# A router's chain rebuilt: logits by token, slots from a triangular matrix, a shorter first gather

## The chip, the cores and the metric

The kernel runs on one core of a Trainium2 chip. The metric is the device time of one execution in microseconds. The engines are TensorE (PE, with PEld for its weight loads), VectorE (DVE), ScalarE (ACT), GpSimd (POOL) and SyncE (SP), which issues the loads of the weights.

## The reference

Two transformer-like blocks run one after the other on 256 tokens of width 1024. The change lies in the first block, between its mixer and its experts:

```python
x = x + merged @ w_o[l]
h = rmsnorm(x, g_ffn[l])
aff = jax.nn.softmax((h @ w_router[l]).astype(f32), axis=-1)     # 256 tokens x 16 experts
vals, idx = lax.top_k(jnp.swapaxes(aff, 1, 2), cap)              # cap = 32 tokens for each expert
xe = h[bidx, idx]
gt = jnp.einsum('becd,edf->becf', xe, w_gate[l])
up = jnp.einsum('becd,edf->becf', xe, w_up[l])
ye = jnp.einsum('becf,efd->becd', jax.nn.silu(gt) * up, w_down[l])
ye = ye * vals[..., None].astype(ye.dtype)
x = x + jnp.zeros_like(x).at[bidx, idx].add(ye.astype(dt))
```

Each of the 16 experts picks its 32 tokens of highest affinity, and three f32 matrices of 1024x2048 (8 MB each) are applied to them. Every weight is read once.

## The kernel before

Tokens lie on partitions, in two tiles of 128; `s.x` holds x as 128 x 2 x 1024. A scheduler places the instructions of each engine in an order of its own; within one engine they then run strictly in that order.

**The end of the mixer.** `w_o(b)` multiplies with one half of w_o's columns, in four pieces, through `lin_A_steps`. Each piece makes 12 matmuls, and the last adds the result to `s.x` (L863). Three pieces into `w_o(1)`, `router_start` and `router_half(0)` come in between: the transposes of x (L896), their copies to `xT` by ScalarE (L897) and VectorE (L898), and the logits (L900). `router_half(1)` does the same for the other four channel tiles once `w_o(1)` is added.

**The router, in `moe`.** The sum of squares and its power -0.5 (`rs`, on POOL, L359) run beside the logits. The logits, 16 x 256 with experts on partitions, are copied (L926) and transposed (L931); softmax (L933 to L942) has tokens on partitions; the affinities are transposed back (L947) and copied (L949). Four rounds of MAX, which finds eight at a time, and three replacements between them (L953, L955) give each expert's 32nd value, the threshold. A token above it gets a slot: two running sums along the tokens (L965), for those above and for those equal to the threshold, are masked and added (L966, L967) and transposed (L970), and `pos` (L972) holds the slot of each token with each expert. `onehot` (L979) compares `pos` with `iota` and makes for each expert two matrices of 128 x 32, for two token tiles: `oh` with rs in it gathers, `wt` with the affinity scatters.

**Gather and experts.** `gather(g, ks, lo, hi)` multiplies the channel tiles `ks` of x with `oh` (L997) and VectorE writes the product times g_ffn to `xe` (L1000). For expert 0 it is called for tiles (0, 1) and (2, 3) first, then the one-hots of all the other experts are written, then the experts run. Expert e takes for each of eight channel tiles k one chunk of w_gate and one of w_up (L1017), then eight chunks of w_down (L1041). In expert 0, `gather` is called for tiles (4, 5) after k=1 and for (6, 7) after k=3, and after w_down for all the other experts.

**The loads.** `wload` (L915, and L919 in two halves) issues on SyncE's queue one DMA for each chunk of 128 x 2048 f32, 1 MB. Its buffers stand in the list `RING2`, 18 of them, with two more (`SPARE`) once. A chunk's load waits until its buffer's last reader is done. The first 20 buffers come free as the mixer ends; load 21 is the first that reuses a buffer of the experts themselves, that of expert 0's w_gate, k=0, and so on in turn: loads 21 to 24 reuse the chunks of k=0 and k=1, load 25 that of w_gate, k=2. Load 43 reuses the buffer of load 25, which is expert 1's w_gate, k=0.

Of the kernel before, what the change touches and what calls it, by code (L numbers as in the profile page):

```python
# [242 lines left out]
class Net:  # L243
# [201 lines left out]
            if next(e[3], StopIteration) is StopIteration:  # L445
                live.remove(e)

    def lin_A_steps(s, aps, xT, kts, evac, cols=512):

        pss = [s.bank([P, cols], name=f"lA{t}") for t in range(2)]  # L450
        n = 0

        def halves():
            for ap in aps or []:
                w = s.wload2(ap, ap.shape[1])
                for a in range(0, ap.shape[1], 2 * cols):
                    yield s.wsplit(w[:, a:a + 2 * cols])
            while aps is None and n < kts:
                yield s.piece()
        for p in halves():  # L460
            h, l = [v.rearrange("p (k c) -> p k c", c=cols) for v in p]
            for i, (w, x) in enumerate(((h, xT[0]), (h, xT[1]), (l, xT[0]))):
                for kk in range(2):
                    for t in range(2):
                        s.nc.tensor.matmul(pss[t], x[:, n + kk, t * P:t * P + P], w[:, kk, :],  # L465
                                           start=n + kk + i == 0, stop=i == 2 and n + kk == kts - 1)
            n += 2
            if n == kts:
                for t in range(2):
                    evac(t, pss[t])  # L470
            yield
# [11 lines left out]
    def mixer(s):  # L483
        nc, A, vec = s.nc, s.A, s.nc.vector
# [38 lines left out]
        r = s.rstd_halves(s.x)  # L523
# [4 lines left out]
        for b in range(2):  # L528
            cs = slice(512 * b, 512 * b + 512)
# [329 lines left out]

        def w_o(b):  # L860
            def evac(t, ps):
                xv = s.x[:, t, 512 * b:512 * b + 512]
                vec.tensor_tensor(xv, xv, ps, op=OP.add)  # L863
            return s.lin_A_steps(None, mm, 8, evac)
        run(w_o(0))
        last = w_o(1)
        for _ in range(3):
# [20 lines left out]
    def router_half(s, b):  # L888

        nc = s.nc  # L890
        for kp in (2 * b, 2 * b + 1):
            ps = s.trb([P, 2, T])
            for j in range(2):
                k = 2 * kp + j
                for t in range(2):
                    nc.tensor.transpose(ps[:, j, t * P:(t + 1) * P], s.x[:, t, k * P:(k + 1) * P], s.ident)  # L896
            nc.scalar.copy(s.xT[:, 2 * kp, :], ps[:, 0, :])  # L897
            nc.vector.tensor_copy(s.xT[:, 2 * kp + 1, :], ps[:, 1, :])  # L898
        for k in range(4 * b, 4 * b + 4):
            nc.tensor.matmul(s.logits, s.gw[:, k, :], s.xT[:, k, :], start=k == 0, stop=k == KT - 1)  # L900

    def moe(s):
        nc, A = s.nc, s.A
# [4 lines left out]
        def wload(ap):  # L908
# [13 lines left out]
        nc.gpsimd.iota(iota, pattern=[[1, C]], base=1, channel_multiplier=0,  # L922
                       allow_small_or_imprecise_dtypes=True)
        r = s.rstd_halves(s.x)
        lg = s.tmp([E, T])
        nc.scalar.copy(lg, s.logits)  # L926


        pl = s.trb([P, 2, E])
        for t in range(2):  # L930
            nc.tensor.transpose(pl[:, t, :], lg[:, t * P:(t + 1) * P], s.ident[:E, :E])  # L931
        mx = s.sm.tile([P, 2], F32, name="mx", bufs=1)
        nc.vector.tensor_reduce(mx, pl, axis=AX, op=OP.max, negate=True)  # L933
        nc.vector.tensor_tensor(mx, mx, r, op=OP.mult)
        aff = s.slot("hsd01", "aff", [P, 2, E], tag="hsd01")
        sm = s.sm.tile([P, 2], F32, name="smx", bufs=1)
        for t in range(2):
            nc.scalar.activation(aff[:, t, :], pl[:, t, :], AF.Exp, scale=r[:, t:t + 1], bias=mx[:, t:t + 1],
                                 accum_out=sm[:, t:t + 1])
        nc.vector.reciprocal(sm, sm)  # L940
        for t in range(2):
            nc.vector.tensor_scalar(aff[:, t, :], aff[:, t, :], sm[:, t:t + 1], None, op0=OP.mult)  # L942
# [13 lines left out]
        thr = m8[:, 7:8]  # L956
        above, equal = [s.tmp([E, 2, T]) for _ in range(2)]
        cnt = s.sm.tile([E, 1], F32, name="cnt", bufs=1)
        ones = s.slot("hsd11", "ones16", [E, T], tag="hsd11")
        nc.gpsimd.memset(ones, 1.0)  # L960
        nc.vector.tensor_scalar(above[:, 0], at, thr, 0.0, op0=OP.is_gt, op1=OP.add, accum_out=cnt)
        nc.vector.tensor_scalar(equal[:, 0], at, thr, None, op0=OP.is_equal)
# [5 lines left out]
        pslot = s.trb([P, 2, E])  # L968
# [3 lines left out]
        nc.vector.tensor_copy(pos, pslot)  # L972

        ohwt = s.slot("K0", "ohwt", [P, 2, 2, E, C])
        oh, wt = ohwt[:, 0], ohwt[:, 1]
# [8 lines left out]
        def gather(g, ks, lo, hi):  # L984

            kk = ks[0] // 4
            if (g, kk) not in xe:
                if g == 0:
                    xe[g, kk] = s.slot("", "xe", [P, 4, 4 * C], tag=("dft", "dft0")[kk])
                else:  # L990
                    both = s.slot(("K1", "X")[g // 3], "xe", [P, 2, 2, 4, 4 * C])
                    xe.update({(i, j): both[:, i - g, j] for i in (g, g + 1) for j in range(2)})
            n = hi - lo
            ps = s.bank([P, len(ks), n * C])
            for i, k in enumerate(ks):
# [14 lines left out]
        for e in range(E):  # L1010
            es = slice(e % 4 * C, (e % 4 + 1) * C)
            pg, pu = s.bank([P, 512]), s.bank([P, 512])
            for k in range(KT):
                for w, ps in (("w_gate", pg), ("w_up", pu)):
                    c = wload(A[w][e, k])
                    for j in range(4):
                        nc.tensor.matmul(ps[32 * j:32 * j + 32, :], xe[e // 4, k // 4][:, k % 4, es],  # L1017
                                         c(j), start=k == 0, stop=k == KT - 1)
                if e == 0 and k in (1, 3):
                    gather(0, (k + 3, k + 4), 0, 1)  # L1020
            pp = s.trb([P, T])
            for t in range(2):
                rep = s.tmp([P, 4, C])
# [838 lines left out]
```

## Time and profile before

| | |
|---|---|
| time, median of 3 runs | 2606.54 us (2606.51 to 2606.96) |
| time of the profiled execution | 2609.32 us |
| its span | 2607.3 us |
| TensorE busy | 2261.8 us, 87% |
| VectorE busy | 1160.5 us, 45% |
| ScalarE busy | 843.2 us, 32% |
| POOL busy | 226.1 us, 9% |
| moved from HBM | 661.92 MB, 254 GB/s over the span |

The profile is that of one execution. Its times count from the start of the span. Busy shares are means over stages of quite different kinds: the mixer ends at about 360 us, the router lies between 360 and 379, the experts follow to about 1290, and the second block takes the rest. TensorE's clock has two levels, and the profile gives the granted share: 1.00 is 2.4 GHz, 0.50 is 1.2 GHz.

### The profile page before, as it was taken

How to read it: one execution, taken by the hardware profiler on the slowest of the kernel's cores; microseconds unless marked ns; L12 is line 12 of the kernel's file. 1: busy time of each engine (PE TensorE's matmuls, PEld its weight loads, DVE VectorE, ACT ScalarE, POOL GpSimd, SP SyncE). 2: the span in 40 equal slices, each digit the busy share in tenths (PEclk: the TensorE clock that was granted, in tenths of full speed). 3: DMA queues.
4: the chain of work that ended last, by engine and by line, in shares of the span. 5: the costliest groups of instructions: out<-in, count | busy, mean ns of one | idle time of the engine just before them, and what ended most of it. 6: DMA issues, size and time to landing. Idle time of an engine off the chain costs nothing.

```text
span 2607.3 us, 33443 instructions
## 1 busy us (share of the span) xinstructions
PE 2261.8 (87%) x13686; PEld 1506.8 (58%) x13686; DVE 1160.5 (45%) x1700; ACT 843.2 (32%) x1299; POOL 226.1 (9%) x250
## 2 busy tenths in 40 slices
PE   7999889767676677677799999999999999989999
PEld 6988854111111111111288887788888888768887
DVE  6886861000000000000265587555555557765554
ACT  4653320000000000000244455355444445545543
POOL 3321300000000000000000041100000005110000
PEclk9999989877778878787799999999999999999999
DMA  5343679999999999999955524245555553424553
GB/s 199 130 146 139 234 281 423 425 426 425 426 425 427 425 426 425 426 425 426 390 195 184 181 96 159 82 162 179 192 179 192 172 175 121 146 80 168 186 180 127
DMA packets 104633, 665.14 MB, mean 255 GB/s; under 512 B 11808, under 2 KB 12192, under 8 KB 34848
## 3 DMA queue, kind: packets, MB, share of 16 engines
q1 hardware_dynamic: 103328, 660.12, 65.4%
q8 instruction: 107, 1.75, 0.3%
q10 hardware_dynamic: 1008, 1.84, 0.2%
q0 software_dynamic: 144, 1.05, 0.1%
q14 instruction: 46, 0.38, 0.0%
HBM read 661.92 MB, written 1.05 MB: 254 GB/s over the span
## 4 chain that ended last, share of the span: by engine, by line
PE 54%; DMA 33%; DVE 8%; ACT 2%; issue 2%; POOL 1%; SPq 0%; DVEq 0%; ACTq 0%; POOLq 0%
PE lA L465 32%; DMA wc<-in_w_down_dram 13%; DMA wc<-in_w_up_dram 13%; PE acc L430 8%; DMA wc<-in_w_gate_dram 5%; PE lA L1670 2%; DVE wl L308 2%; DMA wc<-in_x_wkv_dram 1%; PE trb L1070 1%; ACT wh L307 1%; PE acc L1017 1%; PE acc L313 1%; PE acc L997 1%; PE acc L315 1%; PE acc L314 1%
## 5 line engine op out<-in xcount | busy, mean ns | idle before, releaser
L308 DVE TENSOR_TENSOR wl<-wc,wh 128x1024 fp32r<-128x1024 f32 (+1 forms) x447 | 550.2, 1234 | 376.9 <-ACT wh L307 365.9
L307 ACT CAST wh<-wc 128x1024 fp32r<-128x1024 f32 (+1 forms) x454 | 471.9, 1041 | 553.5 <-PE lA L465 405.2
L1017 PE MATMUL acc<-wc,xe 128*32 128x512 f32 x2048 | 371.1, 769 | 177.1 <-DMA wc<-in_w_up_dram 92.6
L1017 PEld LDWEIGHTS acc<-wc,xe 128*32 128x32 f32 x2048 | 52.5, 120 | 482.4 <-DMA wc<-in_w_up_dram 220.7
L1030 DVE TENSOR_TENSOR tmp<-tmp,acc 128x512 f32<-128x512 f32 x16 | 11.0, 687 | 530.0 <-PE acc L1017 521.8
L465 PE MATMUL lA<-wh,hTl 128*128 128x512 f32 (+1 forms) x864 | 236.4, 390 | 0.0
L465 PE MATMUL lA<-wh,hTh 128*128 128x512 f32 (+1 forms) x864 | 231.3, 388 | 3.4 <-ACT hTh L373 3.4
L465 PE MATMUL lA<-wl,hTh 128*128 128x512 f32 (+1 forms) x864 | 227.8, 385 | 2.6 <-DVE wl L308 2.6
L1041 PE MATMUL acc<-wc,tmp 128*32 128x512 f32 x1024 | 170.0, 745 | 64.4 <-DMA wc<-in_w_down_dram 50.6
L465 PEld LDWEIGHTS lA<-wh,hTh 128*128 128x128 f32 x864 | 161.9, 189 | 35.8 <-ACT hTh L373 5.2
L465 PEld LDWEIGHTS lA<-wl,hTh 128*128 128x128 f32 x864 | 161.9, 189 | 34.0 <-DVE wl L308 3.7
L1029 ACT ACTIVATE tmp<-acc 128x512 f32<-128x512 f32 x16 | 9.6, 597 | 512.6 <-PE acc L1017 512.6
L465 PEld LDWEIGHTS lA<-wh,hTl 128*128 128x128 f32 x864 | 159.0, 189 | 26.5
L1054 DVE TENSOR_TENSOR x<-x,acc 128x512 f32<-128x512 f32 x64 | 44.0, 688 | 263.3 <-PE acc L1053 263.3
L1041 PEld LDWEIGHTS acc<-wc,tmp 128*32 128x32 f32 x1024 | 30.5, 125 | 187.2 <-DMA wc<-in_w_down_dram 100.1
L1050 ACT COPY tmp<-acc 128x512 f32<-128x512 f32 x32 | 18.8, 586 | 313.8 <-PE acc L1041 313.8
L465 PE MATMUL lA<-wl,hidh 128*128 128x512 f32 x352 | 96.1, 391 | 0.0
L465 PE MATMUL lA<-wh,hidh 128*128 128x512 f32 x352 | 94.4, 390 | 0.0
L465 PE MATMUL lA<-wh,hidl 128*128 128x512 f32 x352 | 94.1, 389 | 0.0
L430 PE MATMUL acc<-hTh,wl 128*128 128x256 f32 x544 | 81.1, 290 | 10.4 <-DVE wl L308 10.2
L430 PE MATMUL acc<-hTh,wh 128*128 128x256 f32 x544 | 86.5, 299 | 1.5 <-ACT wh L307 1.0
L1024 POOL COPY tmp<-ohwt 128x128 f32<-128x128 f32 x32 | 9.4, 296 | 847.2 <-PE trb L1033 668.5
(448 smaller groups left out, 3073.1 us busy)
## 6 DMA issues: line engine op xcount, KB each, us to landing
wc<-in_w_up_dram SPq DMA_DIRECT2D x117, 1024.0 KB, 18.4
wc<-in_w_gate_dram SPq DMA_DIRECT2D x102, 1024.0 KB, 19.4
wc<-in_w_down_dram SPq DMA_DIRECT2D x102, 1024.0 KB, 18.3
wc<-in_ffn_wi_dram SPq DMA_DIRECT2D x88, 1024.0 KB, 4.8
wc<-in_ffn_wo_dram SPq DMA_DIRECT2D x40, 1024.0 KB, 4.8
wc<-in_w_in_dram SPq DMA_DIRECT2D x39, 1024.0 KB, 4.8
wc<-in_w_gate_dram SPq DMA_DIRECT2D x52, 512.0 KB, 13.5
wc<-in_w_down_dram SPq DMA_DIRECT2D x52, 512.0 KB, 15.9
```

The source lines that it names most:

```text
L307: s.nc.scalar.copy(h[:, :n], w)
L308: (eng or s.nc.vector).tensor_tensor(l[:, :n], w, h[:, :n].bitcast(F32), op=OP.subtract)
L313: mm(out, a[0], b[0], start=start, stop=False)
L314: mm(out, a[0], b[1], start=False, stop=False)
L315: mm(out, a[1], b[0], start=False, stop=stop)
L430: s.nc.tensor.matmul(ps[:, c, :], w[:, k, :], x[:, k, :], start=i + k == 0, stop=i == len(terms) - 1 and k == KT - 1)
L465: s.nc.tensor.matmul(pss[t], x[:, n + kk, t * P:t * P + P], w[:, kk, :], start=n + kk + i == 0, stop=i == 2 and n + kk == kts - 1)
L997: nc.tensor.matmul(ps[:, i, :], s.x[:, t, k * P:(k + 1) * P], oh[:, t, 4 * g + lo:4 * g + hi].rearrange("p e c -> p (e c)"), start=t == 0, ...
L1017: nc.tensor.matmul(ps[32 * j:32 * j + 32, :], xe[e // 4, k // 4][:, k % 4, es], c(j), start=k == 0, stop=k == KT - 1)
L1041: nc.tensor.matmul(py[b][32 * j:32 * j + 32, :], ht[:, t, 32 * j:32 * j + 32], c(j), start=t == 0, stop=t == 3)
L1054: nc.vector.tensor_tensor(s.x[:, t, cs], s.x[:, t, cs], ps, op=OP.add)
L1670: s.nc.tensor.matmul(pss[t], x[:, n + kk, t * P:t * P + P], w_[:, kk, :], start=n + kk + i == 0, stop=i == 2 and n + kk == KT - 1)
```

## The change

Five things change, all between the mixer's last matmuls and expert 0.

- In the last piece of `w_o(1)` the six matmuls of token tile 0 come first and are added, then those of tile 1, which is added in two halves of 256 columns.
- The logits are computed with tokens on partitions: xT is the stationary operand, the 16 columns of gw the moving one. The copy, the first pair of transposes and the copy of the transposed affinities go away. Softmax runs for one token tile after the other.
- The threshold is transposed and spread over all partitions, and two comparisons write `sel` (above, equal) as bf16 with tokens on partitions. The slots come from products of `sel` with a triangular matrix of ones (`upto`) and a full one, in place of the running sums.
- `iota` moves behind the router's chain, into the buffer of `gw`; its old place is taken by the making of `upto`.
- Before expert 0 only the channel tiles (0, 1) are gathered; (2, 3), (4, 5) and (6, 7) are called after k=0, k=2 and k=4.

```diff
@@ lin_A_steps
+            terms = [(w, x, i, kk) for i, (w, x) in enumerate(((h, xT[0]), (h, xT[1]), (l, xT[0]))) for kk in range(2)]
+            last = in_turn and n + 2 == kts
+            for ts, part in ([((t,), terms) for t in range(2)] if last else [((0, 1), [u]) for u in terms]):
+                for w, x, i, kk in part:
+                    for t in ts:
                         s.nc.tensor.matmul(pss[t], x[:, n + kk, t * P:t * P + P], w[:, kk, :],
                                            start=n + kk + i == 0, stop=i == 2 and n + kk == kts - 1)
+                if last:
+                    evac(ts[0], pss[ts[0]])
@@ router_start
-        s.logits = s.bank([16, T])
+        s.logits = [s.bank([P, 16], name=f"lg{t}") for t in range(2)]
+        s.upto = s.slot("hsd00", "upto", [P, 2, P], BF16, tag="hsd00")
+        nc.gpsimd.memset(s.upto[:, 1], 1.0)
+        ramp = s.slot("hsd01", "ramp", [P, P], tag="hsd01")
+        nc.gpsimd.iota(ramp, pattern=[[1, P]], base=0, channel_multiplier=-1, allow_small_or_imprecise_dtypes=True)
+        nc.gpsimd.tensor_scalar(s.upto[:, 0], ramp, 0.0, None, op0=OP.is_ge)
@@ router_half
-        for k in range(4 * b, 4 * b + 4):
-            nc.tensor.matmul(s.logits, s.gw[:, k, :], s.xT[:, k, :], start=k == 0, stop=k == KT - 1)
+        for t in range(2):
+            for k in range(4 * b, 4 * b + 4):
+                nc.tensor.matmul(s.logits[t], s.xT[:, k, t * P:(t + 1) * P], s.gw[:, k, :], start=k == 0,
+                                 stop=k == KT - 1)
@@ moe
-        iota = s.slot("hsd00", "iota", [P, C], tag="hsd00")
-        lg = s.tmp([E, T])
-        nc.scalar.copy(lg, s.logits)
-        at = s.slot("hsd10", "affT", [E, T], tag="hsd10")
-        nc.scalar.copy(at, pa)
...
-        for v, start in ((above, 0.0), (equal, cnt)):
-            nc.vector.tensor_tensor_scan(v[:, 1], ones, v[:, 0], start, op0=OP.mult, op1=OP.add)
-            nc.vector.tensor_tensor(v[:, 1], v[:, 1], v[:, 0], op=OP.mult)
-        nc.vector.tensor_tensor(above[:, 1], above[:, 1], equal[:, 1], op=OP.add)
...
+        thr = s.trb([P, E])
+        nc.tensor.transpose(thr, m8[:, 7:8].to_broadcast([E, P]), s.ident[:E, :E])
+        for i, op in enumerate((OP.is_gt, OP.is_equal)):
+            nc.vector.tensor_tensor(sel[:, :, i, :], aff, thr.unsqueeze(1).to_broadcast([P, 2, E]), op=op)
+        nc.tensor.matmul(cnt.rearrange("p t i e -> p (t i e)"), upto, sel.rearrange("p t i e -> p (t i e)"),
+                         start=True, stop=False)
+        nc.tensor.matmul(cnt[:, 1].rearrange("p i e -> p (i e)"), total, sel[:, 0].rearrange("p i e -> p (i e)"),
+                         start=False, stop=False)
         for t in range(2):
-            nc.tensor.transpose(pslot[:, t, :], above[:, 1, t * P:(t + 1) * P], s.ident[:E, :E])
+            for u in range(2):
+                nc.tensor.matmul(cnt[:, t, 1, :], total, sel[:, u, 0, :], start=False, stop=t + u == 2)
+        nc.vector.tensor_tensor(num, cnt, sel, op=OP.mult)
+        nc.vector.tensor_tensor(pos, num[:, :, 0], num[:, :, 1], op=OP.add)
+        iota = s.slot("hsd11", "iota", [P, C], tag="hsd11")
...
-        for k in (0, 2):
-            gather(0, (k, k + 1), 0, 1)
+        gather(0, (0, 1), 0, 1)
...
-                if e == 0 and k in (1, 3):
-                    gather(0, (k + 3, k + 4), 0, 1)
+                if e == 0 and k in (0, 2, 4):
+                    gather(0, (k + 2, k + 3), 0, 1)
```

What the scheduler makes of it is seen in the order of the engines. First TensorE, from the gather to the end of expert 0's k=7 (`acc<-ohwt,x` is the gather, `acc<-wc,xe` are the chunks, eight matmuls for each k, `trb<-ident,tmp` the transposes of `wt`). Before:

```order
L997 MATMUL acc<-ohwt,x 128x32 x8
L1025 MATMUL trb<-ident,tmp 128x128 x2
L1017 MATMUL acc<-wc,xe 32x512 x16
L997 MATMUL acc<-ohwt,x 128x32 x4
L1017 MATMUL acc<-wc,xe 32x512 x16
L997 MATMUL acc<-ohwt,x 128x32 x4
L1017 MATMUL acc<-wc,xe 32x512 x32
```

And now:

```order
L1006 MATMUL acc<-ohwt,x 128x32 x4
L1033 MATMUL trb<-ident,tmp 128x128
L1025 MATMUL acc<-wc,xe 32x512 x8
L1006 MATMUL acc<-ohwt,x 128x32 x4
L1025 MATMUL acc<-wc,xe 32x512 x8
L1006 MATMUL acc<-ohwt,x 128x32 x8
L1033 MATMUL trb<-ident,tmp 128x128
L1025 MATMUL acc<-wc,xe 32x512 x48
```

Four matmuls of the gather stand before k=0 instead of eight, and all the others stand between k=0 and k=2.

Then VectorE, from the slots on (`xe<-acc` is the evacuation of a gather, `ohwt` the one-hots, two for each row). Before, with the rows of the experts between left out:

```order
L972 COPY pos<-trb 128x32
L979 TENSOR_SCALAR ohwt<-iota,pos,rs 128x32 x2
L979 TENSOR_SCALAR ohwt<-iota,pos,aff 128x32 x2
L979 TENSOR_SCALAR ohwt<-iota,pos,rs 128x32 x2
L1000 TENSOR_TENSOR xe<-acc,vec_88 128x2x32 x2
...
L979 TENSOR_SCALAR ohwt<-iota,pos,aff 128x32 x2
L1000 TENSOR_TENSOR xe<-acc,vec_88 128x2x32 x2
L1030 TENSOR_TENSOR tmp<-tmp,acc 128x512
```

And now:

```order
L978 TENSOR_TENSOR pos<-num 128x32
L988 TENSOR_SCALAR ohwt<-iota,pos,rs 128x32 x2
L988 TENSOR_SCALAR ohwt<-iota,pos,aff 128x32 x2
L1009 TENSOR_TENSOR xe<-acc,vec_88 128x2x32
...
L988 TENSOR_SCALAR ohwt<-iota,pos,aff 128x32 x2
L1009 TENSOR_TENSOR xe<-acc,vec_88 128x2x32 x3
L1038 TENSOR_TENSOR tmp<-tmp,acc 128x512
```

One evacuation stands ahead of the rows left out and three behind them, where there were two and two; between them stand 30 rows of two one-hots, where there were 29.

Last POOL, from the last product of the second block's gains to the copies of `wt`, before:

```order
L1812 TENSOR_TENSOR gfg<-vec_88,vec_0_3107 128x8
L359 TENSOR_TENSOR rs<-ms,neghalf 128x2
L960 MEMSET ones_3165 16x256
L1024 COPY tmp<-ohwt 128x128 x32
```

And now:

```order
L1820 TENSOR_TENSOR gfg<-vec_88,vec_0_3122 128x8
L980 IOTA iota 128x32
L359 TENSOR_TENSOR rs<-ms,neghalf 128x2
L1032 COPY tmp<-ohwt 128x128 x32
```

`iota` stands ahead of `rs`, and since its buffer is that of `gw` it waits for the last matmul of the logits.

## Rows read from the trace of the kernel before

**Rows 1.** The page: span, and the DMA line of its 40 slices.

```profile
span 2607.3 us, 33443 instructions
DMA  5343679999999999999955524245555553424553
```

**Rows 2.** Windows: busy time of PE, PEld, DVE, ACT, POOL, then PEclk, DMA share, GB/s.

```profile
372.00:374.00 2.00, 0.18 (x2) 0.21 (x2) 1.64 (x4) 0.00 (x0) 0.00 (x0) 0.50 0.04 16
...
380.00:382.00 2.00, 2.00 (x12) 0.39 (x8) 2.00 (x11) 0.00 (x0) 0.00 (x0) 0.50 0.25 33
382.00:384.00 2.00, 2.00 (x20) 0.44 (x12) 2.00 (x11) 0.00 (x0) 0.00 (x0) 0.84 0.79 311
500.00:1290.00 790.00, 550.00 (x2747) 102.29 (x2743) 55.72 (x81) 29.90 (x57) 8.17 (x26) 0.79 1.01 426
```

**Rows 3.** Timeline of SyncE's queue: start, us, what, count of issues merged.

```profile
380.84 3.90 SPq L915 DMA_DIRECT2D wc<-in_w_down_dram  x4
...
386.40 0.33 SPq L915 DMA_DIRECT2D wc<-in_w_gate_dram  x1
```

**Rows 4.** Timeline of PE; a matmul in f32 shows as two passes.

```profile
378.84 5.50 PE L1017 MATMUL acc<-wc,xe 128*32 128x512 f32 x32
384.27 1.08 PE L997 MATMUL acc<-ohwt,x 128*128 128x32 f32 x8
385.27 3.64 PE L1017 MATMUL acc<-wc,xe 128*32 128x512 f32 x32
...
426.24 6.21 PE L1017 MATMUL acc<-wc,xe 128*32 128x512 f32 x56
```

**Rows 5.** The chain that ended last, 359 to 392: start, us, what.

```profile
359.42 1.30 DVE x L863 x2
...
361.77 1.94 PE acc L900 x8
...
365.03 0.12 ACT aff L938
...
366.45 0.39 PE trb L947 x2
...
366.86 0.37 ACT affT L949
...
367.25 0.43 DVE m L953
...
370.59 0.48 DVE tmp L961 x2
...
374.22 0.20 DVE pos L972
...
374.45 0.31 DVE ohwt L979
...
374.80 3.64 PE acc L997 x16
...
378.47 0.22 DVE xe L1000
378.69 11.99 DVE ohwt L979 x58
...
390.86 1.47 PE acc L1017 x9
```

**Rows 6.** Timeline of POOL around the iota and the power.

```profile
231.38 0.17 POOL L922 IOTA iota<- 128x32 f32 x1 [10.43 <-PE acc L314]
...
362.65 0.73 POOL L359 TENSOR_TENSOR rs<-ms,neghalf 128x2 f32<-128x2 f32 x1 [49.68 <-DVE ms L357]
```

**Rows 7.** Windows of half a microsecond where the granted clock falls and rises.

```profile
292.00:292.50 0.50, 0.14 (x2) 0.00 (x0) 0.50 (x2) 0.00 (x0) 0.50 (x1) 1.00 0.00 0
297.00:297.50 0.50, 0.00 (x0) 0.00 (x0) 0.50 (x2) 0.00 (x0) 0.50 (x1) 0.80 0.81 328
382.50:383.00 0.50, 0.50 (x8) 0.12 (x4) 0.50 (x4) 0.00 (x0) 0.00 (x0) 0.87 0.70 262
```

More of the change, by code (lines that the diff above doesn't have):

```diff
@@ L446, in braid, with lin_A_steps @@
                 live.remove(e)
-    def lin_A_steps(s, aps, xT, kts, evac, cols=512):
+    def lin_A_steps(s, aps, xT, kts, evac, cols=512, in_turn=False):
         pss = [s.bank([P, cols], name=f"lA{t}") for t in range(2)]
@@ L461, in lin_A_steps @@
             h, l = [v.rearrange("p (k c) -> p k c", c=cols) for v in p]
-            for i, (w, x) in enumerate(((h, xT[0]), (h, xT[1]), (l, xT[0]))):
-                for kk in range(2):
-                    for t in range(2):
+            terms = [(w, x, i, kk) for i, (w, x) in enumerate(((h, xT[0]), (h, xT[1]), (l, xT[0]))) for kk in range(2)]
[3 more added lines that the diff above has]
+                    for t in ts:
                         s.nc.tensor.matmul(pss[t], x[:, n + kk, t * P:t * P + P], w[:, kk, :],
                                            start=n + kk + i == 0, stop=i == 2 and n + kk == kts - 1)
+                if last:
+                    evac(ts[0], pss[ts[0]])
             n += 2
-            if n == kts:
+            if n == kts and not last:
                 for t in range(2):
@@ L861, in evac @@
             def evac(t, ps):
-                xv = s.x[:, t, 512 * b:512 * b + 512]
-                vec.tensor_tensor(xv, xv, ps, op=OP.add)
-            return s.lin_A_steps(None, mm, 8, evac)
+                for c in range(0, 512, 256 if b and t else 512):
+                    cs = slice(c, c + (256 if b and t else 512))
+                    xv = s.x[:, t, 512 * b:512 * b + 512][:, cs]
+                    vec.tensor_tensor(xv, xv, ps[:, cs], op=OP.add)
+            return s.lin_A_steps(None, mm, 8, evac, in_turn=b == 1)
         run(w_o(0))
@@ L920, in wload @@
             return lambda j: ts[j // 2][:, 512 * (j % 2):512 * (j % 2) + 512]
-        iota = s.slot("hsd00", "iota", [P, C], tag="hsd00")
-        nc.gpsimd.iota(iota, pattern=[[1, C]], base=1, channel_multiplier=0,
-                       allow_small_or_imprecise_dtypes=True)
         r = s.rstd_halves(s.x)
-        lg = s.tmp([E, T])
-        nc.scalar.copy(lg, s.logits)
-        pl = s.trb([P, 2, E])
-        for t in range(2):
-            nc.tensor.transpose(pl[:, t, :], lg[:, t * P:(t + 1) * P], s.ident[:E, :E])
         mx = s.sm.tile([P, 2], F32, name="mx", bufs=1)
-        nc.vector.tensor_reduce(mx, pl, axis=AX, op=OP.max, negate=True)
-        nc.vector.tensor_tensor(mx, mx, r, op=OP.mult)
         aff = s.slot("hsd01", "aff", [P, 2, E], tag="hsd01")
         sm = s.sm.tile([P, 2], F32, name="smx", bufs=1)
[L937 to L942, printed above, removed]
         pa = s.trb([E, T])
         for t in range(2):
+            one = lambda v: v[:, t:t + 1]
+            nc.vector.tensor_reduce(one(mx), s.logits[t], axis=AX, op=OP.max, negate=True)
+            nc.vector.tensor_tensor(one(mx), one(mx), one(r), op=OP.mult)
+            nc.scalar.activation(aff[:, t, :], s.logits[t], AF.Exp, scale=one(r), bias=one(mx), accum_out=one(sm))
+            nc.vector.reciprocal(one(sm), one(sm))
+            nc.vector.tensor_scalar(aff[:, t, :], aff[:, t, :], one(sm), None, op0=OP.mult)
             nc.tensor.transpose(pa[:, t * P:(t + 1) * P], aff[:, t, :], s.ident)
-        at = s.slot("hsd10", "affT", [E, T], tag="hsd10")
-        nc.scalar.copy(at, pa)
         wk = s.tmp([E, T])
@@ L955, in moe @@
                 nc.vector.match_replace(out=wk, in_to_replace=m8, in_values=wk if i else pa, imm_value=-1.0)
[L956 to L962, printed above, removed]
@@ L964, in moe @@
-        for v, start in ((above, 0.0), (equal, cnt)):
-            nc.vector.tensor_tensor_scan(v[:, 1], ones, v[:, 0], start, op0=OP.mult, op1=OP.add)
-            nc.vector.tensor_tensor(v[:, 1], v[:, 1], v[:, 0], op=OP.mult)
-        nc.vector.tensor_tensor(above[:, 1], above[:, 1], equal[:, 1], op=OP.add)
-        pslot = s.trb([P, 2, E])
+        thr = s.trb([P, E])
+        nc.tensor.transpose(thr, m8[:, 7:8].to_broadcast([E, P]), s.ident[:E, :E])
+        sel = s.slot("hsd10", "sel", [P, 2, 2, E], BF16, tag="hsd10")
@@ new lines, in moe @@
+        for i, op in enumerate((OP.is_gt, OP.is_equal)):
+            nc.vector.tensor_tensor(sel[:, :, i, :], aff, thr.unsqueeze(1).to_broadcast([P, 2, E]), op=op)
+        upto, total = s.upto[:, 0], s.upto[:, 1]
+        cnt = s.trb([P, 2, 2, E])
+        nc.tensor.matmul(cnt.rearrange("p t i e -> p (t i e)"), upto, sel.rearrange("p t i e -> p (t i e)"),
+                         start=True, stop=False)
+        nc.tensor.matmul(cnt[:, 1].rearrange("p i e -> p (i e)"), total, sel[:, 0].rearrange("p i e -> p (i e)"),
+                         start=False, stop=False)
@@ L969, in moe @@
         for t in range(2):
-            nc.tensor.transpose(pslot[:, t, :], above[:, 1, t * P:(t + 1) * P], s.ident[:E, :E])
+            for u in range(2):
+                nc.tensor.matmul(cnt[:, t, 1, :], total, sel[:, u, 0, :], start=False, stop=t + u == 2)
+        num = s.sm.tile([P, 2, 2, E], F32, name="num", bufs=1)
+        nc.vector.tensor_tensor(num, cnt, sel, op=OP.mult)
         pos = s.sm.tile([P, 2, E], F32, name="pos", bufs=1)
-        nc.vector.tensor_copy(pos, pslot)
+        nc.vector.tensor_tensor(pos, num[:, :, 0], num[:, :, 1], op=OP.add)
@@ L974, in moe @@
+        iota = s.slot("hsd11", "iota", [P, C], tag="hsd11")
+        nc.gpsimd.iota(iota, pattern=[[1, C]], base=1, channel_multiplier=0,
+                       allow_small_or_imprecise_dtypes=True)
         ohwt = s.slot("K0", "ohwt", [P, 2, 2, E, C])
```

## The prediction

> **What bounds the kernel now.** I read the slices first: the DMA line of [rows 1] stands at 9 from slice 7 to slice 20, where the kernel streams the experts' weights. The windows say what that stretch is worth: from 500 to 1290 the DMA share is 1.01 at 426 GB/s, while TensorE is busy 550 of 790 us [rows 2]. So the transfers set the end of this stage, and one load of 128x2048 f32 (1.049 MB) takes 1.049/0.426 = 2.46 us. What the router's chain can win or lose is the time for which these transfers stand still ahead of it: 16 GB/s in 372:374, 33 in 380:382, 311 in 382:384 [rows 2]. SyncE's timeline gives the reason [rows 3]: every buffer is full, and the four loads that begin at 380.84 need the chunks of expert 0's k=0 and k=1. TensorE begins k=0 at 378.84 [rows 4], at half clock (0.50 in 380:382), so the first load is issued 2.00 us after that. By 384.0 there have arrived 2 x 33 + 2 x 311 = 688 KB, 1.6 us of work at 426 GB/s: the transfers stand as if they had begun at full rate at 382.4, 1.55 us after the issue. From there on nothing stops them in this stage.
>
> So I read the chain of waits [rows 5] from the last addition of w_o, 359.42, to that restart. It is one file of small steps in which TensorE has little to do.
>
> **The chain, step by step.** *x to logits.* Before: additions from 359.42, transposes, copies, eight passes in 1.94 us, end at 361.77 + 1.94 = 363.71 [rows 5]. After: the addition of token tile 0 runs under the matmuls of tile 1, and tile 1 is added in halves of about 1.30/4 = 0.33 us, so the transposes stand about 1.30 - 0.33 - 0.07 = 0.9 us earlier, and the logits with them, from 360.9. They now load xT as weights: 16 passes of 16 columns. Nearest row: the gather at full clock, 8 passes of 32 columns in 1.08 us [rows 4], some 0.12 apart with a tail of 0.1 to 0.2. 16 of them take 1.95, the end is 362.85. Bounds: no gain at all if 16 passes took 0.17 each, 1.3 us if VectorE's copies were the later ones. I take 0.85.
>
> *Logits to Exp.* Before 1.32 us (363.71 to 365.03 [rows 5]). Out go ScalarE's copy and two transposes. But POOL's file has changed: iota, whose buffer was gw's, waits for the last logit and stands ahead of rs, behind which VectorE's scaled maximum waits, and Exp. Before, rs ran at 362.65 under the logits and took 0.73, iota 0.17 [rows 6]. After: 0.05 + 0.17, 0.05 + 0.73, and about 0.3 for the scaling and Exp's start: 1.3, so Exp begins at 364.15 and nothing is gained here; with rs ahead of iota it would be 0.7 more.
>
> *Exp to first MAX.* Before 2.22 us (365.03 to 367.25). Out goes the copy affT, 0.37 and its waits of 0.04, and tile 0's reciprocal and scaling slide under tile 1's Exp, about 0.2. So 365.75. The four MAX and three replacements are the same 3.34 us (367.25 to 370.59), to 369.1.
>
> *MAX to first one-hot.* Before 3.86 us (370.59 to 374.45). After: a transpose of the threshold, 0.45 with its waits (L947's pair took 0.39); two comparisons of 0.2, L972's length; six products with 128x128 bf16 weights, which no row shows. Lower bound 0.1 each, L947's pair with 16 weight columns being 0.39 in all; upper bound the gather's 3.64/16 = 0.23 at half clock. I take 0.15, since few columns pass through: 1.2 us with waits of 0.3; bounds 0.9 and 1.7. Then product and sum, 0.3 and 0.25, as L972 to L979 (0.23). The sum is 2.6 to 2.7, so the first one-hot begins at 371.8 against 374.45: **2.65 us earlier**; with both lower terms 1.3, with both upper ones 3.4. By the Trainium skill (TensorE: Matmul & The Clock Gate, LDWEIGHTS) a load of 128 weight columns is an estimated 0.11 us whatever the operand's height, which would put the one-hot 0.2 us earlier; no row here shows such a load in bf16.
>
> *The gather.* Only tiles (0, 1) go first: 8 passes, not 16. First matmul 0.35 after the one-hot (374.45 to 374.80), the evacuation 8 x 0.23 plus a tail of 0.1 later, at 374.1; before, that of the second pair stood at 378.47. One transpose follows on TensorE, so k=0 begins at 374.4, 4.45 us earlier than 378.84; the first load is issued at 376.4, and the transfers stand as from 377.95.
>
> **What is late next.** The order shows what the diff doesn't: on VectorE the evacuation of channel tiles (2, 3) stands behind 60 one-hots. 58 of them take 11.99 us, 0.207 each [rows 5]; 60 take 12.4. TensorE is in order and waits for that evacuation at k=2. Before, the same queue held back k=4 only, to 390.86, 0.18 after the one-hots' end (378.69 + 11.99). So k=2 begins at 374.1 + 0.22 + 12.4 + 0.18 = 386.9. The loads for the buffers of k=0 and k=1 last 4 x 2.46 = 9.85 us, to 387.8. The fifth needs gate k=2, which at full clock is done and answered 1.13 us after its start (385.27 to 386.40 [rows 3, 4]), and flows 1.55 later: 386.9 + 2.7 = 389.6. So the transfers stop a second time, for 1.8 us. Before, the fifth load's turn was at 382.4 + 9.85 = 392.25. Hence the sum: first restart 4.45 us earlier, second stop 1.8, **net 2.65 us**. Afterwards a chunk frees a buffer every 3.64/4 = 0.91 us against 2.46 for a load, and no third stop follows. In short: the one-hots begin 2.65 us earlier, and the fifth load hangs on them by fixed lengths; the four loads before it only fill the wait.
>
> Edits at nothing: the triangular matrix's three POOL instructions stand where iota stood at 231.38, after 10.43 us without work [rows 6]; without that cover they would cost up to three times rs's 0.73. On SyncE's queue no load moves past another but for the three of w_down ahead of the first stop: the one that waits for the logits is now first of them. Issued at 362.9, they land by 362.9 + 1.55 + 3 x 2.46 = 371.8, still ahead of the restart. The first half of the logits lies among w_o's matmuls with as much PE time as before.
>
> **The clock.** TensorE had worked until 292.14; its granted clock was 1.00 in 292:292.5 and 0.80 in the mean of 297:297.5 [rows 7], the fall from 2.4 to 1.2 GHz 5 us after the work's end. It was back in 382.5:383, 8 us after the gather of 374.80 had begun. With the change TensorE is idle about 3 us before k=2, so I count k=2 at full clock. The Trainium skill (TensorE: Matmul & The Clock Gate, HAM oscillation) warns of just such waits between bursts, after which each burst begins at half rate; by it k=2 would begin at half clock. The trace agrees that idling lowers the clock, but only after a longer pause.
>
> **Rivals.** *A, forecast (0.60):* as above. The profiled execution had a span of 2607.3 and a time of 2609.3, 2.8 over the median; the shift is a difference within it and goes on the median: 2606.5 - 2.65 = 2603.9. *B (0.14):* k=2 begins at half clock, and the fifth load is issued 2.00, not 1.13, after it: 0.87 later, 2604.8. For it: a pause soon after a cold start. Against: the 5 us of [rows 7]. *C (0.12):* there is no second stop, since k=2 comes earlier than I think, or the products are cheap and the clock hasn't fallen for the gather (0.11 less for each of 8 passes): 4.5 to 5.6 us, 2600.9 to 2602.0. Against: 0.207 us is steady over 58 one-hots, and the clock stood at 0.50 in 372:374. *E (0.09):* the change shortens the chain little, since rs now follows iota and products and logits cost their upper bounds: 1.3 us, 2605.2. *D, slower (0.05):* the clock stays at half through expert 0 after the pause at k=2. Its twelve remaining chunks and its eight of w_down take 0.87 us more each, 17.4 us. Load 18 after the fifth, due at 389.6 + 18 x 2.46 = 433.9 and so to be issued by 432.3, needs the buffer of expert 1's first chunk. Before, expert 1 began at 426.24 [rows 4], and with k=2 to k=7 at full clock it begins some 0.7 earlier, so that buffer comes free near 426.7, 5.6 us in hand. A loss of 17.4 makes a third stop of 11.8: 2615.7. It decides from a loss of 5.6 us in expert 0; the kernel is slower than before from 8.3, and by over 0.2% from 13.5. Against: the clock was back within 8 us of steady work.
>
> **How the numbers follow.** Two tenths of a percent, 5.2 us, is about what a measurement of this kernel can tell from no change. A, B and E lie within it, and half of C; beyond it lie C's other half, 0.06, a hundredth for what I haven't thought of, and D: faster 0.07, same 0.88, slower 0.05. The range takes in A with its bounds of 1.3 and 3.4, B with a chain half a microsecond worse, E and nearly all of C: 2601.0 to 2605.8.
>
> **What would show it.** One-hots begin near 371.8 and k=0 near 374.4; VectorE's three evacuations stand together near 386.7, with TensorE idle some 3 us before; SyncE issues four loads from 376.4 and the fifth near 388; the DMA share shows two dips, the second of about 2 us; rs begins after the logits' end. I am wrong if logits wait for copies, if the products take more than 1.7 us, if k=2 begins at half clock, or if the transfers stand still later in the stage.

## The result, and the profile after

The changed kernel takes 2630.03 us (median of 4 runs, 2627.93 to 2631.09) against 2606.53 for the kernel before (4 runs, 2606.26 to 2606.96): 1.0089 of it, with a 95% interval of 1.0072 to 1.0106. It is 23.5 us slower; the prediction was 2603.9.

The router's chain was shortened nearly as forecast. The loss arises in stages whose instructions the change doesn't touch. I read the trace from the router outward, and first the chain that ended last (start, us, what), against [rows 5]:

```profile
357.71 0.43 DVE x L870
...
359.20 1.99 PE lg L914 x16
361.19 0.06 issue
361.25 0.16 POOL iota L980
361.41 0.70 POOL rs L359
...
362.32 0.46 ACT aff L947 x2
...
363.96 0.43 DVE m L956
...
366.85 0.43 DVE m L956
...
367.41 0.27 PE trb L961
367.70 0.30 DVE sel L964 x2
...
368.05 0.24 PE trb L968
368.28 0.03 PE trb L970
368.31 0.11 PE trb L974 x4
...
368.92 0.31 DVE ohwt L988
...
371.23 0.23 DVE xe L1009
371.46 12.39 DVE ohwt L988 x60
383.85 0.14 DVE xe L1009
383.99 0.04 issue
384.04 6.34 PE acc L1025 x37
```

The one-hots begin at 368.92, 5.53 us earlier than the 374.45 before. The last row of the sixty and what follows it are the second stall that the prediction named: TensorE's k=2 waits for the evacuation behind them. SyncE's queue, against [rows 3]:

```profile
373.51 4.47 SPq L930 DMA_DIRECT2D wc<-in_w_down_dram  x4
386.03 0.33 SPq L930 DMA_DIRECT2D wc<-in_w_gate_dram  x1
```

Four loads begin 2.00 us after k=0 (371.51), the fifth is issued at 386.03, 1.99 us after k=2. The windows, against [rows 2], show both stops, the clock at half when k=2 starts, and in the last row the first thing that was not expected:

```profile
372.00:374.00 2.00, 2.00 (x12) 0.39 (x8) 2.00 (x11) 0.00 (x0) 0.00 (x0) 0.50 0.04 8
374.00:376.00 2.00, 2.00 (x20) 1.12 (x16) 2.00 (x11) 0.00 (x0) 0.00 (x0) 0.96 0.67 205
...
380.00:381.00 1.00, 0.00 (x0) 0.00 (x0) 1.00 (x6) 0.98 (x2) 0.00 (x0) 1.00 0.99 393
381.00:381.50 0.50, 0.00 (x0) 0.00 (x0) 0.50 (x4) 0.40 (x1) 0.00 (x0) 0.50 1.13 475
...
382.00:384.00 2.00, 0.00 (x0) 0.00 (x0) 2.00 (x11) 0.00 (x0) 0.00 (x0) 0.50 1.03 430
384.00:386.00 2.00, 1.96 (x12) 0.59 (x16) 0.24 (x2) 0.00 (x0) 0.00 (x0) 0.50 0.72 303
386.00:388.00 2.00, 2.00 (x12) 0.39 (x8) 0.00 (x0) 0.00 (x0) 0.00 (x0) 0.55 0.50 94
...
500.00:1290.00 790.00, 547.39 (x2736) 100.54 (x2728) 55.99 (x82) 29.59 (x57) 8.18 (x26) 0.79 1.01 423
```

From 500 to 1290 the DMA engines are as busy as before (1.01) and move 423 GB/s, not 426. The fifth load flows from 386.03 + 1.55 = 387.6, by 4.65 us earlier than the 392.25 before. When the second block starts, little of that is left. TensorE's timeline there, before (`acc<-wc,tmp` is a chunk of w_down, eight matmuls; the row at 1285.12 is the last of the sixteen experts'):

```profile
1285.12 1.06 PE L1041 MATMUL acc<-wc,tmp 128*32 128x512 f32 x8 [1.14 <-DMA wc<-in_w_down_dram]
1286.89 3.55 PE L1053 MATMUL acc<-tmp 128*128 128x512 f32 x4 [0.71 <-ACT tmp L1050]
...
1292.12 0.74 PE L465 MATMUL lA<-wh,hTh 128*128 128x512 f32 x2 [1.09 <-ACT hTh L373]
...
1303.88 1.08 PE L465 MATMUL lA<-wh,hTh 128*128 128x512 f32 x4
1304.80 1.07 PE L465 MATMUL lA<-wh,hTl 128*128 128x512 f32 x4
1305.70 1.07 PE L465 MATMUL lA<-wl,hTh 128*128 128x512 f32 x4
```

and after, with the first chunks of expert 0, which answer to [rows 4], ahead of it:

```profile
371.51 3.21 PE L1025 MATMUL acc<-wc,xe 128*32 128x512 f32 x16
...
384.04 8.49 PE L1025 MATMUL acc<-wc,xe 128*32 128x512 f32 x60 [4.40 <-DVE xe L1009]
...
1285.96 1.06 PE L1049 MATMUL acc<-wc,tmp 128*32 128x512 f32 x8 [1.26 <-DMA wc<-in_w_down_dram]
1287.73 1.98 PE L1061 MATMUL acc<-tmp 128*128 128x512 f32 x4 [0.71 <-ACT tmp L1058]
...
1291.39 0.73 PE L468 MATMUL lA<-wh,hTh 128*128 128x512 f32 x2 [1.05 <-ACT hTh L373]
...
1304.08 1.09 PE L468 MATMUL lA<-wh,hTl 128*128 128x512 f32 x4
1305.01 1.09 PE L468 MATMUL lA<-wl,hTh 128*128 128x512 f32 x4
1305.94 1.09 PE L468 MATMUL lA<-wh,hTl 128*128 128x512 f32 x4
```

The last chunk of the experts waits for its load in both, and begins 0.84 us later than before (1285.96 against 1285.12): between the fifth load and the last one the transfers gave back all of the 4.65 us and 0.84 more, 5.5 in all. The rows at 1292.12 and 1291.39 are the third and fourth matmul of the second block in both, and here the changed kernel is 0.73 us ahead again: the four matmuls behind the last chunk took 3.55 us before, at a granted clock of 0.54 (1287 to 1289), and 1.98 now, at 1.00. That is the clock of one execution and nothing that the change does: in a run of the old router further down, b_all256, the same four took 1.98. The rows from 1303.88 and 1304.08 on are the same kind of matmul in the same order, at the same granted clock (1.00). Four of them follow the four before every 0.93 us (1304.08, 1305.01, 1305.94), where it was 0.91 in the mean of 0.92 and 0.90 (1303.88, 1304.80, 1305.70). Over longer rows of such starts it is 0.2333 us for one (1304.08 to 1316.21, 52 of them) against 0.2266 (1304.80 to 1316.58). In the second block 6 groups of such rows count 3 x 768 + 3 x 352 = 3360 matmuls; 3360 x 6.7 ns = 22.5 us. The span grew by 20.8, and with the 0.73 by which the row at 1291.39 is earlier, 21.5 us were lost behind it. So the second block's loss is its 128x512 matmuls, each 3% dearer.

What can do that to instructions that nobody changed? In the first block w_o's matmuls already had the longer distance (333.10, 334.04, 334.97, 335.90), ahead of the router's first instruction on TensorE (351.77); of the new router only the making of `upto` on POOL lies before them (229.04 to 230.16). So it was neither the clock after the second stop nor anything that the router does behind w_o. The theory I formed is where the operands lie. The pools stand one behind another in a partition, and `sm` lost `cnt` (4 bytes, 32 with its rounding) and got `num`, 2 x 2 x 16 f32 = 256 bytes. All that is allocated behind `sm` moved up by 224 bytes. From the two programs' allocations, first byte and its remainder to 256:

```
pool    what it holds                              before       after
ring    loaded weights                             31232   0    31232   0
spl     wh and wl, the matmuls' moving operands    64000   0    64000   0
t2      temporaries                                91136   0    91360 224
phmix   mixer and experts: weights, mh, xT, xe    101376   0   101600 224
late    hTh and hTl, the stationary operands      101376   0   101600 224
```

The kernel has tiles in it that nothing reads, among them one of 128x112 f32 in `sm`; making it larger or smaller moves the addresses and leaves every instruction as it is. The rivals: the new instructions themselves (lin_A's rewritten loop, a second bank for the logits), and the stall ahead of k=2.

### The profile page after: what moved, and what is told of

It reads as the page before. It is cut to its first block, busy times and chain, and to the rows that moved or that the text cites. A ratio compares the mean times of both kernels' runs of the same rounds, so it can differ in the third digit from the quotient of the medians.

```text
span 2628.1 us, 33475 instructions
## 1 busy us (share of the span) xinstructions
PE 2279.9 (87%) x13705; PEld 1502.9 (57%) x13705; DVE 1156.0 (44%) x1699; ACT 840.8 (32%) x1297; POOL 227.2 (9%) x252
## 4 chain that ended last, share of the span: by engine, by line
PE 55%; DMA 32%; DVE 8%; ACT 2%; issue 1%; POOL 1%; SPq 0%; DVEq 0%; ACTq 0%; POOLq 0%
PE lA L468 33%; DMA wc<-in_w_up_dram 12%; DMA wc<-in_w_down_dram 10%; DMA wc<-in_w_gate_dram 9%; PE acc L430 7%; PE lA L1678 3%; DVE wl L308 2%; PE acc L1049 1%; PE trb L1078 1%; PE acc L1025 1%; PE acc L313 1%; DMA wc<-in_ffn_wi_dram 1%; ACT wh L307 1%; PE acc L570 1%; PE acc L1006 1%
## 5 line engine op out<-in xcount | busy, mean ns | idle before, releaser
L430 PE MATMUL acc<-hTh,wl 128*128 128x256 f32 x544 | 80.2, 288 | 11.1 <-DVE wl L308 10.7
L430 PE MATMUL acc<-hTh,wh 128*128 128x256 f32 x544 | 85.6, 297 | 1.5 <-ACT wh L307 1.0
```

The costliest lines, as they stand in the source:

```text
L430: s.nc.tensor.matmul(ps[:, c, :], w[:, k, :], x[:, k, :], start=i + k == 0, stop=i == len(terms) - 1 and k == KT - 1)
```

## The experiments

**a_pad8: the changed kernel with its old addresses.**

```diff
-        s.sm.tile([P, 112], F32, name="even", bufs=1)
+        s.sm.tile([P, 120], F32, name="even", bufs=1)
```

> The changed kernel with one unused tile of 128x112 f32 made 128x120, so that every tile allocated behind the small tiles of the pool sm moves up by 32 bytes per partition. In the changed kernel the new tile num (256 bytes) in place of cnt (32 with its rounding) moved them by 224 bytes, and 224 + 32 = 256. Theory: the loss is that shift, by which the operands' addresses (multiples of 256 before) are no multiples of 64 any more. Then the 128x512 matmuls of lin_A return from 0.933 to 0.906 us for four, the experts' loads from 423 to 426 GB/s, and the shortened router remains: 4 to 6 us below before, 2600.5 to 2602.5. Rival 1: the new instructions (the rewritten loop of lin_A, the second logits bank) cost the time: 0.933 stays and the time is 2630. Rival 2, half clock and the second stop of the transfers cost it: 2630 as well, with the loss ahead of 390 us.

It took 2606.91 us, 0.9995 of before (0.9986 to 1.0004). Thirty-two bytes in each partition that hold nothing gave back 23 us. The experts' loads run at 426 GB/s again, and lin_A's matmuls show

```profile
1304.16 1.08 PE L468 MATMUL lA<-wh,hTh 128*128 128x512 f32 x4
1305.08 1.07 PE L468 MATMUL lA<-wh,hTl 128*128 128x512 f32 x4
1305.99 1.07 PE L468 MATMUL lA<-wl,hTh 128*128 128x512 f32 x4
```

Both rivals fall: the instructions and the stall are all still there. But the 4 to 6 us that I expected from the router are not. I had read them off the changed kernel's trace (4.65 at the fifth load), in which w_o also ended 1.94 us earlier (357.67 against 359.61), and that is nothing the router does. Less that, it is 2.7, and the interval (3.6 below before to 1.0 above) holds 2.7.

The traces say a little more, if the last chunk of the experts is counted from w_o's end. Before it begins 925.5 us after it (1285.12 less 359.61), in a_pad8 923.8 (1286.99 less 363.23): 1.7 us less, though in this execution w_o ended 3.6 us later than before.

**b_224, b_64, b_128, b_ring32: the kernel before with only its addresses moved.** The unused tile larger by 224, 64 or 128 bytes moves all that stands behind `sm`; the last one moves `ring` and `spl` instead, and leaves the rest.

```diff
b_224, b_64, b_128:
-        s.sm.tile([P, 112], F32, name="even", bufs=1)
+        s.sm.tile([P, 168], F32, name="even", bufs=1)     # or 128, 144
b_ring32:
+        s.pad = pool("pad", 1)
+        s.pad.tile([P, 8], F32, name="pad", bufs=1)
         s.ring = pool("ring", 4)
...
-        s.sm.tile([P, 112], F32, name="even", bufs=1)
+        s.sm.tile([P, 104], F32, name="even", bufs=1)
```

> The kernel before with the unused tile 128x112 f32 made 128x168: the tiles behind sm move up by 224 bytes, to the very addresses that they have in the changed kernel; no instruction differs. Theory (placement): lin_A's matmuls go from 0.906 to 0.933 us for four, worth about 21.5 us in the second block, and the experts' loads from 426 to 423 GB/s, worth 790 x 3/426 = 5.6 us; in all 2633, with 2628 to 2638 as bounds. Rival (the instructions cost it): 2606.5, within 2.

> The kernel before with the unused tile made 128x128: the tiles behind sm move up by 64 bytes. If what counts is a multiple of 64 bytes, 2606.5 and 0.906 us for four matmuls. If it is a multiple of 128 or 256, slower, up to the 2633 expected of a shift by 224. If the instructions cost the time, 2606.5 too; only together with the shift by 224 does this run say which.

> The kernel before with the tiles behind sm moved up by 128 bytes; a shift by 64 cost 24 us. If a multiple of 128 bytes is enough for both operands of a matmul, 2606.6 and 0.906 us for four; if it takes 256, about 2631 and 0.933.

> The kernel before with an unused tile of 32 bytes ahead of the pools ring and spl and the other unused tile 32 bytes smaller: only ring and spl (weights as loaded in the second block, and their halves wh and wl, the matmuls' moving operands) move by 32 bytes; sm and all behind it, with the stationary operands hTh, hTl and hid, stay. In the changed kernel it was the other way round. If the stationary operand's place sets the 0.933, nothing changes here: 2606.5. If any operand off a multiple of 64 bytes does it, 0.933 again and some 20 us more, 2627.

**b_all64, b_all128, b_all256: everything behind `const` moved together.** `const` is the first pool in a partition, and `ring` stands behind it. As in b_ring32 an unused tile, here of 64, 128 or 256 bytes, stands ahead of `ring`, and the one in `sm` keeps its size.

> The kernel before with an unused tile of 64 bytes ahead of the pools ring and spl: all buffers of both matmul operands move by 64 bytes together. Shifting those behind sm alone by 64 or ring and spl alone by 32 cost 24 to 25 us. If each operand's own address counts, slow here too, 0.933 and 2631 or more. If it is how the two stand to each other (stationary against moving), fast, 0.906 and 2606.6.

> As b_all64, which kept lin_A's matmuls at 0.906 but moved the experts' weights at 419 GB/s, with 128 bytes in place of 64. Matmuls, whose two operands stand to each other as before: 0.906. Transfers: if their destination needs a multiple of 128 bytes, 426 and 2606.5; if one of 256, 419 and 790 x 7/426 = 13 us more, 2619.5.

> The kernel before with an unused tile of 256 bytes ahead of ring and spl: all buffers behind const move by 256 bytes together. A control: if addresses count by their remainder to 256, this is the kernel before in all respects: 0.906 us for four matmuls, 426 GB/s in the experts, 2606.5. If the extra tile or the absolute place does something of its own, it shows here as a difference of more than 2 us.

But for after and a_pad8, which stand there to compare, all of these are the old router, instruction for instruction (times of before on the same chips: 2606.47 to 2606.76):

| | moved by (bytes) | mean ns, lA<-wh,hTh | GB/s, 500 to 1290 | time, us | to before (95%) |
|---|---|---|---|---|---|
| before | | 392 | 426 | 2606.5 | |
| after | behind sm, 224 | 396 | 423 | 2630.03 | 1.0072 to 1.0106 |
| b_224 | behind sm, 224 | 396 | 423 | 2632.25 | 1.0079 to 1.0107 |
| b_64 | behind sm, 64 | 396 | 424 | 2630.64 | 1.0073 to 1.0100 |
| b_128 | behind sm, 128 | 396 | 424 | 2630.76 | 1.0073 to 1.0104 |
| b_ring32 | ring and spl, 32 | 396 | 424 | 2631.53 | 1.0075 to 1.0102 |
| b_all64 | all, 64 | 391 | 419 | 2622.01 | 1.0043 to 1.0070 |
| b_all128 | all, 128 | 391 | 419 | 2622.33 | 1.0040 to 1.0067 |
| b_all256 | all, 256 | 391 | 426 | 2607.51 | 0.9993 to 1.0011 |
| a_pad8 | behind sm, 256 | 391 | 426 | 2606.91 | 0.9986 to 1.0004 |

The mean of one grows by 4 or 5 ns, the distance between starts by up to 6.7. TensorE's timeline of b_224 in the second block:

```profile
1304.10 1.10 PE L465 MATMUL lA<-wh,hTl 128*128 128x512 f32 x4
1305.04 1.10 PE L465 MATMUL lA<-wh,hTh 128*128 128x512 f32 x4
```

and that of b_all64 in w_o:

```profile
338.13 1.07 PE L467 MATMUL lA<-wh,ml 128*128 128x512 f32 x4
339.04 1.07 PE L467 MATMUL lA<-wl,mh 128*128 128x512 f32 x4
```

b_224 reproduces the whole loss without a line of the change: 25.6 us, 0.94 from start to start. With b_ring32, where the moving operands were shifted and the stationary ones not, 0.93 comes too. With b_all64, where both were shifted alike, it is 0.91 as before. So for these matmuls it isn't an operand's own address that counts but how far the stationary and the moving one stand from each other: a multiple of 256 bytes costs nothing, 32, 64 and 224 off it cost 6.7 ns, and 128 off it a little less, 5.7 (b_128: 0.2323 us for one, 1306.23 to 1319.24, 56 of them). What it is in the chip that makes this distance count, no run shows.

b_224 has the changed kernel's addresses and the old router, so the difference between these two is the router alone: 2630.03 against 2632.25 us, 2.2 less. Their intervals overlap, but the traces agree with it:

```profile
1291.19 1.06 PE L1041 MATMUL acc<-wc,tmp 128*32 128x512 f32 x8 [1.24 <-DMA wc<-in_w_down_dram]
```

In b_224 the last chunk of the experts begins 930.6 us after w_o's end (1291.19 less 360.55), in the changed kernel 928.3 (1285.96 less 357.67).

b_all64's windows show why it is slower all the same:

```profile
500.00:1290.00 790.00, 538.65 (x2702) 97.63 (x2706) 54.40 (x79) 26.66 (x52) 7.70 (x26) 0.80 1.02 419
```

Does 419 for 426 explain its 15.5 us? 790 x 7/426 = 13.0, and from 400 to 500 it is 419 for 424, another 1.2: nearly all of it. Here the buffers' own address counts, and a shift of 128 is no better than one of 64; 256 restores it. In the kernels where some of the experts' buffers moved it is 423 or 424. The Trainium skill (DMA: Bandwidth & Descriptors, How a descriptor splits into AXI transactions) says that a transfer which doesn't start on a multiple of 256 bytes begins with a transaction from the multiple below its start. By it, an estimate for a row of 8 KB is 33 transactions instead of 32, 3%; the runs agree on the 256 and measure 1.6%, and that this is the mechanism isn't shown: the page speaks of the side that is read, and here the side that is written was moved.

**a_old_gather: the rebuilt chain with the old gather, on the old addresses.**

```diff
-        gather(0, (0, 1), 0, 1)
+        for k in (0, 2):
+            gather(0, (k, k + 1), 0, 1)
...
-                if e == 0 and k in (0, 2, 4):
-                    gather(0, (k + 2, k + 3), 0, 1)
+                if e == 0 and k in (1, 3):
+                    gather(0, (k + 3, k + 4), 0, 1)
```

> The changed kernel on multiples of 256 bytes (as a_pad8), with the gather as before: channel tiles (0, 1) and (2, 3) first, then (4, 5) after k=1 and (6, 7) after k=3. So the rebuilt chain alone. In a_pad8 k=0 began 14.1 us after the last addition of w_o's start against 19.4 in the kernel before, of which the shorter first gather gives 8 passes at half clock, 1.9 us; here about 16.0, so k=0 3.4 us earlier than before, no second stop of the transfers, and 2603.1 against 2606.5. Rival: the chain's gain is lost elsewhere in the stage, as a_pad8: 2606.9.

2604.22 against 2606.76 us, 0.9987 (0.9978 to 0.9996). From w_o's end (360.12) to k=0 (375.85) it takes 15.7 us; before it was 19.2 (359.61 to 378.84). The chain alone is worth 3.5 us there and 2.5 of the time; that the shorter first gather adds to it, a_pad8 gives no sign.

**a_late_oh and a_late_iota: the second stop and POOL's wait taken away.** Both on the old addresses; the first writes the other experts' one-hots after expert 0's last gather, the second also gives `iota` a buffer in `sm`, so that it is made at the program's start.

```diff
-        for e in range(E):
-            if e:
-                onehot(oh, lambda t: r[:, t:t + 1], e)
-            onehot(wt, lambda t: aff[:, t, e:e + 1], e)
...
                 if e == 0 and k in (0, 2, 4):
                     gather(0, (k + 2, k + 3), 0, 1)
+                if e == 0 and k == 4:
+                    for f in range(E):
+                        onehot(wt, lambda t: aff[:, t, f:f + 1], f)
+                        if f:
+                            onehot(oh, lambda t: r[:, t:t + 1], f)
```

> The changed kernel with its addresses on multiples of 256 bytes again (as in the run a_pad8), and the one-hots of the other experts written after expert 0's last gather, not ahead of its second, so that the evacuations for k=2 to k=7 stand behind none of them. In a_pad8's trace TensorE waited 3.57 us for xe ahead of k=2 at half clock, and from 390 to 400 the transfers moved 2 x 311 + 8 x 295 = 2982 KB where 426 GB/s make 4260: 3.0 us lost. Theory: that second stop goes, and the time is 3.0 us below a_pad8's, some 2.7 below before: 2603.9 against 2606.6. Rival: the transfers' stop is hidden or comes back when expert 0's down projection waits behind the 60 one-hots: no change to a_pad8, 2606.9.

> As a_late_oh, and iota has a small buffer of its own and is written at the program's start, so that on POOL nothing waits for the last logit ahead of rs; addresses behind sm are on multiples of 256 again. In a_pad8 the scaled maximum waited 0.74 us for rs after the row maxima were there. Theory: the chain is another 0.7 us shorter, 2603.2. Rival: the logits' end sets it (iota isn't the wait), as a_late_oh.

2603.04 us, 0.9988 (0.9980 to 0.9997), and 2602.51 us, 0.9983 (0.9974 to 0.9992), against 2606.47 on the same chip. As expected in both, though between them 0.5 is within what their runs scatter. The windows of a_late_oh:

```profile
372.00:374.00 2.00, 1.95 (x11) 0.59 (x14) 1.74 (x9) 0.00 (x0) 0.00 (x0) 0.50 0.04 8
...
376.00:378.00 2.00, 2.00 (x19) 1.07 (x22) 1.20 (x7) 0.00 (x0) 0.00 (x0) 1.00 0.80 328
378.00:380.00 2.00, 2.00 (x24) 0.52 (x16) 2.00 (x11) 0.00 (x0) 0.00 (x0) 1.00 0.97 365
...
382.00:384.00 2.00, 2.00 (x24) 0.65 (x20) 2.00 (x11) 0.00 (x0) 0.00 (x0) 1.00 1.03 434
...
386.00:388.00 2.00, 2.00 (x20) 0.53 (x17) 2.00 (x11) 0.00 (x0) 0.00 (x0) 1.00 1.03 434
```

One stop of the transfers, no second one, and TensorE at full clock throughout k=2 to k=7 (1.00 in every window from 376 to 392). In a_late_iota POOL runs `rs` ahead of the logits' end:

```profile
361.94 0.73 POOL L359 TENSOR_TENSOR rs<-ms,neghalf 128x2 f32<-128x2 f32 x1 [48.91 <-DVE ms L357]
```

and from the logits' end (360.85 + 1.97 = 362.82) to the first one-hot (369.83) it takes 7.01 us, in a_late_oh 7.75 (362.20 to 369.95): the 0.7 that the prediction put on `rs` standing behind `iota`. This kernel is the best of all, 4 us below before and 27 below the changed one. Counted from w_o's end the last chunk of the experts begins 4.9 us earlier than before in a_late_oh and 5.2 in a_late_iota (920.6 and 920.3 us against 925.5), more than the 3.4 and 4.0 that reach the time. In both traces the second block takes longer than before; why, no run shows.

## Why the prediction was wrong

The step that failed is "Edits at nothing". It named three edits that move work and missed one that moves no work: `num` in place of `cnt` in `sm`. I took it that what stands outside the router's section runs as before, since its instructions and their order are the same. 224 bytes made 3360 matmuls of the second block 6.7 ns dearer and the experts' loads 0.7% slower, 21.5 and 5.5 us in the traces. That was shown from both sides: put back in the changed kernel (a_pad8), put into the old one (b_224). The hundredth that I left for what I hadn't thought of was far too little and stood on the wrong side, in the 0.07 for a faster kernel; and of the rivals the only one on the slow side, D, went by another mechanism, which didn't occur: the clock was back at 1.00 in 388 to 390.

The router's steps, in the trace of the changed kernel, from w_o's end, since that moved by itself:

- *x to logits*, gain 0.85 taken: 3.52 us (357.67 to 361.19) for 4.10 (359.61 to 363.71), so 0.6. The sixteen passes took 1.97 and 1.95 was forecast.
- *Logits to Exp*, 1.3: 1.13. `iota` does stand ahead of `rs`, as the order showed.
- *Exp to MAX* 1.6: 1.64. *The MAX rounds* 3.34: 3.32.
- *MAX to one-hot* 2.65: 1.64 (367.28 to 368.92). The mis-sized term is the six products. I took 0.15 each and 1.2 with their waits; the rows from 368.05 to 368.42 show 0.37 in all, less than my lower bound. The loads of their weights, which I had estimated at 0.11 each, lie within 0.27 us for all six (368.04 to 368.31 on PEld). My nearest rows were f32, two passes each.
- *One-hot to k=0* 2.6: 2.59. *k=0 to k=2* 12.5: 12.53, the sixty one-hots 12.39 of 12.4. *The second stop* came where it was forecast.
- *The clock:* I counted k=2 at full clock, and it ran at 0.50 (384 to 386): rival B. TensorE had come back to full clock in 374 to 376 (0.96) and then stood for 4.40 us, from 379.64 on. The granted clock was 1.00 in 380 to 381 and 0.50 in 381 to 381.5, so here it fell less than 2 us after the work's end, where [rows 7] had shown 5: one fall was too little to say that only a longer pause lowers it. It costs the 0.87 us that B put on it: the fifth load is issued 1.99 us after k=2, not 1.13. The Trainium skill (TensorE: Matmul & The Clock Gate, HAM oscillation), which I had weighed and set aside by my reading of [rows 7], says that a burst behind such a wait starts at half clock, and the trace agrees (0.50 in 384 to 386).

So the chain was 3.6 us shorter, not 2.65, and B took 0.87 of it: 2.7 us net, by luck what was forecast. With the addresses equal, the changed kernel and b_224 lie 2.2 us apart in their times and 2.3 in the experts' stage, a_pad8 and before 1.7 in that stage; the times of a_pad8 alone can't tell 2.7 from nothing. The three kernels without the second stop gain 2.5 (a_old_gather), 3.4 (a_late_oh) and 4.0 us (a_late_iota): they show that the shorter chain pays, and not the forecast's net.

Two things stay open. Why w_o ended 1.94 us earlier in the changed kernel's trace, I didn't settle. The start of w_o, 334.31 before and 332.17 in the changed kernel, lies in single executions anywhere from 331.88 (b_64) to 338.26 (a_pad8). A part may be the mixer's 128x256 matmuls, for which the shift is a small gain: 0.1183 us from start to start in b_224 (329.98 to 334.71, 40 of them) against 0.1200 before (330.47 to 334.31, 32). Some 1250 of them stand ahead of w_o, 2 us by an estimate from these rows. And the loads at 423 and 424 with part of the buffers shifted are not in proportion to their number.

## What to carry to other kernels

When a change adds or drops a tile, work out what it does to the addresses of all that is allocated behind it: a few bytes in a pool of small tiles can cost more than the edit brings. A loss spread evenly over instructions that the change doesn't touch, at the same clock and in the same order, points to where the data lie, and a tile that nobody reads, grown by a few bytes, settles it. And a forecast by steps, however good each step is, needs the question what else the edit shifts: ports, banks, addresses.

## What the runs showed of the hardware

- A 128x512 matmul of this kernel in fp32r follows the one before by 0.2266 us if its stationary and moving operands stand a multiple of 256 bytes apart in the partition, by 0.2333 if they are 32, 64 or 224 bytes off that, and by 0.2323 if 128, at the same granted clock of 1.00. The 128x256 ones of L430, whose stationary operand lies in `spl` and whose moving one behind `sm`, show no such cost: a mean of 299 ns before and 297 after for acc<-hTh,wh, and 0.1200 us from start to start before against 0.1183 in b_224.
- Loads of 128x2048 f32 into buffers that start on a multiple of 256 bytes came at 426 GB/s, into buffers 64 or 128 bytes off it at 419, with the DMA engines as busy (1.01, 1.02).
- Six bf16 products with 128x128 weights and 16 to 64 moving columns took 0.37 us together at a granted clock of 0.50 (368 to 368.5), where eight f32 passes of 32 columns take 1.92 (369.28).
